# Splitting every second weight unit of the merged stage with ScalarE and an adding transfer in place of VectorE

## The chip, the cores and the metric

The kernel runs on one core of a Trainium2 chip. The metric is the device time of one execution in microseconds. The core has TensorE (PE in the profile, with its weight loads as PEld), VectorE (DVE), ScalarE (ACT), GpSimd (POOL) and SyncE (SP). Each works through its own queue of instructions in order, and they wait for each other through semaphores. Transfers are issued from a queue (here from SP's, ScalarE's or GpSimd's) and carried out by 16 DMA engines that all queues share.

## The reference

One decoder layer on 256 tokens of width 2048, all in float32. The part that matters here is the end, in which two branches are projected, gated and merged:

```python
h = _rmsnorm(x, pre_norm_g)
proj = jnp.einsum('bsd,de->bse', h, w_in)
...                                     # attention -> attn, short convolution -> conv
y_mla = jnp.einsum('bse,ed->bsd', attn, w_o_mla)
y_conv = jnp.einsum('bse,ed->bsd', b_gate * conv * jax.nn.silu(z_conv), w_o_conv)
merged = jax.nn.sigmoid(g_mla) * y_mla + jax.nn.sigmoid(g_conv) * y_conv
out = jnp.einsum('bsd,de->bse', merged, w_out)
x = x + _rmsnorm(out, post_norm_g)
```

g_mla and g_conv are column blocks of proj. The four products that make merged are each 256 x 2048 by 2048 x 2048.

## The kernel before

TensorE multiplies operands of the type float32r, a float32 that is rounded to fewer bits. To keep the precision each operand is split in two: hi is the rounded value and lo = value - hi, rounded too. A product is then three matmuls, hi times hi, hi times lo and lo times hi (`product`, line 227). Weights are split on the chip, once each.

Weights come in units, numbered in the order of their use (`plan`). A unit is 128 x 2048 float32, 1024 KB. `load_raw` issues its load on SP's queue into one of three raw buffers. `split_unit` splits it in two halves of 1024 columns: `split_act` (line 244) has ScalarE write hi (a copy with rounding, line 245) and VectorE write lo = raw - hi (line 246). The halves lie in five buffers for hi (tag whi) and five for lo (tag wlo). `ahead` and `take` keep loads up to three units and splits one unit ahead of the unit that TensorE uses; on the chip the buffers decide how far ahead the work really runs.

The merged stage is the loop `for c in range(4)` at line 967. For each block of 512 output columns c there are four products n: the two gates (left operand x_both, the normalised input), the attention branch (at_both) and the convolution branch (cv_both). Each product takes four units (`tokens`, line 941), and a unit serves both token tiles t and four slices k4 of 128 rows: first the four slices for t = 0, then the four for t = 1, 24 matmuls. The first half of a unit holds slices 0 and 1, the second half slices 2 and 3. In all 64 units (`u_d`), with the numbers 113 to 176. After n = 3 of each block VectorE gates and adds the two branches, transposes the result in blocks of 32, and GpSimd's queue writes it to device memory (eight DMAs far<-sg, line 328) and reads it back (two DMAs sg<-far, line 332), from where it is split into m_both, an operand of the last stage. The names of the tiles carry the unit: raw131 is the raw tile of unit 131, wlo131_1024 the low part of its second half.

TensorE's order is fixed by program order. Instructions inside `keep_in_program_order` keep theirs on their engine too; a scheduler places the others.

Of the kernel before, what the change touches and what calls it, by code (L numbers as in the profile page):

```python
# [11 lines left out]
F32 = mybir.dt.float32  # L12
F32R = mybir.dt.float32r
I32 = mybir.dt.int32
AF = mybir.ActivationFunctionType
ALU = mybir.AluOpType
# [66 lines left out]
def tile_layer(ctx: ExitStack, tc: tile.TileContext, xw, w0, xb, x, pos, pvec, post_g, wc, wz, wcv, wkr, wqk, wqr, wv, cwr, wsq, out):  # L83
    nc = tc.nc
# [21 lines left out]
    def add(ap, width=UNIT):  # L106
        plan.append((ap, width))
        return len(plan) - 1
# [30 lines left out]
    u_d = [[[add(wsq[n, c, k]) for k in range(4)] for n in range(4)] for c in range(4)]  # L139
# [3 lines left out]
    u_out = {ck: add(wsq[4, ck[0], ck[1]]) for ck in out_order}  # L143
# [4 lines left out]
    def load_raw(i):  # L148
# [16 lines left out]
        if i == u_ckv[1]:  # L165
            tc.keep_in_program_order(nc.sync.dma_start(out=x_tok, in_=x))

    def split_unit(i):
        t, w = raws.pop(i), plan[i][1]
        parts = []  # L170
        if i == u_kr:
            t = t[:, :w].rearrange("p (k c) -> p k c", k=KD)
            for h in range(2):
                both = wpool.tile([P, HALF], F32R, name=f"whi{i}_{h}", tag="whi", bufs=5)
                both = both[:, :].rearrange("p (k j c) -> p k j c", k=KD // 2, j=2)
                ks = slice(h * KD // 2, (h + 1) * KD // 2)
                split_act(both[:, :, 0], both[:, :, 1], t[:, ks])
                parts.append(both.rearrange("p k j c -> p k (j c)"))
            splits[i] = parts
            return  # L180
        if i <= u_qa[-1]:

            hi, lo = (wpool.tile([P, HALF], F32R, name=f"{o}{i}", tag=o, bufs=5) for o in ("whi", "wlo"))
            for j in range(2):
                k, o = 2 * i + j, j * XW
                src = x_first if k == 0 else t[:, o : o + S]
                split_scaled(x_both, src, k)
                split_act(hi[:, j * R : (j + 1) * R], lo[:, j * R : (j + 1) * R], t[:, o + S : o + XW], True)
            splits[i] = [(hi, lo)]
            return  # L190
        for h in range(0, w, HALF):
            n = min(HALF, w - h)
            if u_out[3, 0] <= i < u_out[3, 3]:
                hi, lo = (op.tile([P, HALF], F32R, name=f"w{o}{i}_{h}") for o in ("hi", "lo"))
            else:
                hi = wpool.tile([P, HALF], F32R, name=f"whi{i}_{h}", tag="whi", bufs=5)
                lo = wpool.tile([P, HALF], F32R, name=f"wlo{i}_{h}", tag="wlo", bufs=5)
            split_act(hi[:, :n], lo[:, :n], t[:, h : h + n], i == u_head[0][1], i in (u_grp["r", 0], u_grp["v", 0], u_head[0][0]))
            parts.append((hi, lo))
        splits[i] = parts  # L200

    def ahead(i, raw=3, split=1):
        while done["raw"] < min(i + raw, len(plan)):
            load_raw(done["raw"])
            done["raw"] += 1
        while done["split"] < min(i + 1 + split, len(plan)):
            while done["raw"] <= done["split"]:
                load_raw(done["raw"])
                done["raw"] += 1
            split_unit(done["split"])  # L210
            done["split"] += 1
# [32 lines left out]
    def split_act(hi, lo, src, keep=False, later=False):  # L244
        a = nc.scalar.activation(hi, src, AF.Copy)  # L245
        b = nc.vector.tensor_tensor(lo, src, hi.bitcast(F32), op=ALU.subtract)  # L246
        if keep:

            tc.keep_in_program_order(a)
        if keep or later:  # L250
            tc.keep_in_program_order(b)
# [52 lines left out]
    n = 2 * XW // S  # L304
# [38 lines left out]
    def split_scaled(dst, src, k):  # L343
        if k < 3:

            a = nc.vector.tensor_scalar(dst[:, k, :S], src, col("pre_g", k), None, op0=ALU.mult)
        else:
            a = nc.scalar.activation(dst[:, k, :S], src, AF.Copy, scale=col("pre_g", k))
        tc.keep_in_program_order(a)
        tc.keep_in_program_order(  # L350
            nc.vector.scalar_tensor_tensor(
                dst[:, k, S:], src, col("pre_g", k), dst[:, k, :S].bitcast(F32), op0=ALU.mult, op1=ALU.subtract
            )
        )
# [839 lines left out]
```

## Time and profile before

| | before |
|---|---|
| median of two runs | 1034.59 us (1034.59 and 1034.60) |
| span of the profiled execution | 1032.9 us |
| its time beside the span | 1.7 us of the run lie outside it |
| merged stage (589.95 to 938.15 us) | 348.20 us |
| mean granted clock of TensorE | 0.999 |
| VectorE, ScalarE, GpSimd busy in the merged stage | 192.78, 156.29, 22.24 us |
| DMA share in the merged stage | 0.58 |

Times are from the start of the span. A row of a timeline reads: start, duration, engine, line of the kernel, operation, out<-in, shapes, count, and in brackets the idle time ahead of it with what ended it. A row of waits reads: engine, what it was about to do, what it waited for, total us, times, longest. A row of DMA queues reads: packets, MB, share of the 16 engines' time; a row of DMA issues: what, from which queue, count, KB each, median us from issue to landing. The line numbers are those of the kernel before; in the changed kernel everything behind the change stands 11 lines further down.

### The profile page before, as it was taken

The numbers are of one execution on the slowest core, as the hardware profiler recorded it, in microseconds if no ns is written. First come the engines' busy times: TensorE is split into PE (matmuls) and PEld (weight loads), VectorE is DVE, ScalarE is ACT, GpSimd is POOL, SyncE is SP. The second block draws the span as 40 slices with busy tenths as digits, with TensorE's granted clock in tenths as the row PEclk, the third lists the DMA queues.
The fourth block names the chain that finished last, engine by engine and source line by source line (L and its number), as shares of the span: only waits on it lengthen the run. The fifth ranks groups of instructions, "written<-read, shape, count | busy, mean of one in ns | idle before, by whom it ended". The sixth has DMA issues, their size and how long they took to land.

```text
span 1032.9 us, 12670 instructions
## 1 busy us (share of the span) xinstructions
PE 1026.4 (99%) x4648; PEld 854.6 (83%) x4648; DVE 687.9 (67%) x973; ACT 531.3 (51%) x750; POOL 174.2 (17%) x324
## 2 busy tenths in 40 slices
PE   9999999999999999999999999999999999999997
PEld 8888888888888888888888888888888888888886
DVE  7588777787687777777777785564455455455562
ACT  7675555655456464564555465344434444443551
POOL 4620421104210223112133120020010001002000
PEclk9999999999999999999999999999999999999999
DMA  9775766558675676857676765565565556558642
GB/s 356 280 257 214 269 215 227 207 191 297 212 252 193 209 279 210 278 184 242 229 271 222 267 217 200 204 222 188 201 218 208 188 202 243 183 187 335 231 165 81
DMA packets 44669, 233.24 MB, mean 226 GB/s; under 512 B 7968, under 2 KB 10656, under 8 KB 21696
## 3 DMA queue, kind: packets, MB, share of 16 engines
q1 hardware_dynamic: 32544, 199.67, 54.4%
q0 software_dynamic: 11632, 29.48, 8.9%
q10 hardware_dynamic: 432, 3.29, 0.8%
q8 instruction: 36, 0.59, 0.2%
q14 instruction: 25, 0.20, 0.1%
HBM read 215.66 MB, written 12.58 MB: 221 GB/s over the span
## 4 chain that ended last, share of the span: by engine, by line
PE 99%; DVE 0%; ACT 0%; issue 0%
PE cv L88 34%; PE sq L88 34%; PE z L88 8%; PE out L88 8%; PE qa L88 2%; PE kn L88 2%; PE qn L88 2%; PE vv L88 2%; PE ckv L88 2%; PE qr L88 1%; PE o L88 1%; PE sw L88 1%; PE sc L88 1%; PE idle L88 0%; PE kr L88 0%; DVE og L1048 0%
## 5 line engine op out<-in xcount | busy, mean ns | idle before, releaser
L246 DVE TENSOR_TENSOR wlo<-raw,whi 128x1024 fp32r<-128x1024 f32 (+1 forms) x370 | 440.5, 1196 | 276.6 <-ACT whi L245 265.5
L245 ACT ACTIVATE whi<-raw 128x1024 fp32r<-128x1024 f32 (+1 forms) x372 | 382.7, 1035 | 412.2 <-PE sq L88 180.5
L88 PE MATMUL cv<-whi,x_both 128*128 128x512 f32 x1024 | 319.8, 389 | 0.0
L88 PEld LDWEIGHTS cv<-whi,x_both 128*128 128x128 f32 x1024 | 192.3, 188 | 39.6
L88 PE MATMUL cv<-wlo,x_both 128*128 128x512 f32 x512 | 199.4, 390 | 0.0
L88 PE MATMUL sq<-whi,x_both 128*128 128x512 f32 x512 | 158.2, 389 | 0.0
L88 PEld LDWEIGHTS sq<-whi,x_both 128*128 128x128 f32 x512 | 96.1, 188 | 19.8
L88 PEld LDWEIGHTS cv<-wlo,x_both 128*128 128x128 f32 x512 | 96.1, 188 | 19.3
L88 PE MATMUL sq<-wlo,x_both 128*128 128x512 f32 x256 | 99.6, 389 | 0.0
L88 PE MATMUL z<-whi,x_both 128*128 128x512 f32 x256 | 80.0, 389 | 0.0
L88 PE MATMUL sq<-whi,at_both 128*128 128x512 f32 x256 | 79.4, 389 | 0.0
L88 PE MATMUL sq<-whi,cv_both 128*128 128x512 f32 x256 | 79.4, 389 | 0.0
L88 PE MATMUL out<-whi,m_both 128*128 128x512 f32 x256 | 79.0, 389 | 0.0
L328 POOL DMA_DIRECT2D far<-sg x32 | 17.5, 553 | 305.8 <-DVE sg L320 232.6
L328 POOL DMA_DIRECT2D far<-via x64 | 35.2, 557 | 191.4 <-DVE via L320 190.0
L88 PEld LDWEIGHTS sq<-wlo,x_both 128*128 128x128 f32 x256 | 48.1, 188 | 10.0
L88 PEld LDWEIGHTS out<-whi,m_both 128*128 128x128 f32 x256 | 48.1, 188 | 10.0
L88 PEld LDWEIGHTS sq<-whi,cv_both 128*128 128x128 f32 x256 | 48.1, 188 | 9.9
L88 PEld LDWEIGHTS sq<-whi,at_both 128*128 128x128 f32 x256 | 48.1, 188 | 9.9
L88 PEld LDWEIGHTS z<-whi,x_both 128*128 128x128 f32 x256 | 48.1, 188 | 9.9
L88 PE MATMUL z<-wlo,x_both 128*128 128x512 f32 x128 | 49.8, 389 | 0.0
L88 PE MATMUL sq<-wlo,at_both 128*128 128x512 f32 x128 | 49.8, 389 | 0.0
(227 smaller groups left out, 1131.3 us busy)
## 6 DMA issues: line engine op xcount, KB each, us to landing
raw<-wsq_dram SPq DMA_DIRECT2D x80, 1024.0 KB, 4.8
raw<-wcv_dram SPq DMA_DIRECT2D x64, 1024.0 KB, 5.5
raw<-wz_dram SPq DMA_DIRECT2D x16, 1024.0 KB, 4.8
raw<-wqk_dram SPq DMA_DIRECT2D x8, 1024.0 KB, 6.1
cw<-cwr_dram POOLq DMA_DIRECT2D x24, 256.0 KB, 5.8
raw<-wc_dram SPq DMA_DIRECT2D x4, 1024.0 KB, 9.8
raw<-wv_dram SPq DMA_DIRECT2D x4, 1024.0 KB, 5.3
far<-via POOLq DMA_DIRECT2D x64, 48.0 KB, 4.1
```

What stands on the lines that cost most here:

```text
L88: return tc.keep_in_program_order(nc.tensor.matmul(*a, **kw))
L245: a = nc.scalar.activation(hi, src, AF.Copy)
L246: b = nc.vector.tensor_tensor(lo, src, hi.bitcast(F32), op=ALU.subtract)
L328: tc.keep_in_program_order(queue.dma_start(out=f[i], in_=m))
```

## The change

In the merged stage the units with an odd number (113, 115, ... 175, the first and third of each product) are split in another way. ScalarE writes hi as before, then a second ScalarE instruction writes lo = -hi, and a DMA from GpSimd's queue adds the raw columns onto lo within SBUF: lo = -hi + raw. VectorE has no part in it. The units with an even number and all other stages stay as they are. 

```diff
+    def by_transfers(i):
+
+        return u_d[0][0][0] <= i < u_out[0, 0] and i % 2 == 1
+
     def split_unit(i):
...
                 hi = wpool.tile([P, HALF], F32R, name=f"whi{i}_{h}", tag="whi", bufs=5)
                 lo = wpool.tile([P, HALF], F32R, name=f"wlo{i}_{h}", tag="wlo", bufs=5)
+            if by_transfers(i):
+                src = t[:, h : h + n]
+                nc.scalar.activation(hi[:, :n], src, AF.Copy)
+                nc.scalar.activation(lo[:, :n], hi[:, :n].bitcast(F32), AF.Copy, scale=-1.0)
+                tc.keep_in_program_order(nc.gpsimd.dma_start(out=lo[:, :n], in_=src, accum_op=ALU.add))
+                parts.append((hi, lo))
+                continue
             split_act(hi[:, :n], lo[:, :n], t[:, h : h + n], i == u_head[0][1], i in (u_grp["r", 0], u_grp["v", 0], u_head[0][0]))
             parts.append((hi, lo))
```

GpSimd's queue at the end of the first column block (c = 0, after unit 128) held only the writes and the reads back of the merged tiles before, from this block to the next:

```order
L328 DMA far_6181<-sg1_0_5883 32x4x128 x4
L328 DMA far_6185<-sg1_1_5885 32x4x128 x4
L332 DMA sg0_0_5733<-far_6181 128x512
L332 DMA sg0_1_5735<-far_6185 128x512
L328 DMA far_6765<-sg1_0_6480 32x4x128 x4
```

The same place now, with the adding transfers (line 206) of units 129 to 133 round it:

```order
L206 DMA wlo129_0_6163<-raw129_6126 128x1024
L206 DMA wlo129_1024_6168<-raw129_6126 128x1024
L339 DMA far_6199<-sg1_0_5893 32x4x128 x4
L339 DMA far_6203<-sg1_1_5895 32x4x128 x4
L343 DMA sg0_0_5739<-far_6199 128x512
L343 DMA sg0_1_5741<-far_6203 128x512
L206 DMA wlo131_0_6253<-raw131_6216 128x1024
L206 DMA wlo131_1024_6258<-raw131_6216 128x1024
L206 DMA wlo133_0_6323<-raw133_6286 128x1024
```

The transfers of units 131, 147 and 163 now stand behind the writes and reads back of a block, and those of units 129, 145 and 161 ahead of them.

ScalarE's queue in the same part of the program, before (units 128 to 130):

```order
L245 ACTIVATE whi128_1024_6116<-raw128_6076 128x1024
L245 ACTIVATE whi129_0_6146<-raw129_6110 128x1024
L245 ACTIVATE whi129_1024_6150<-raw129_6110 128x1024
L245 ACTIVATE whi130_0_6200<-raw130_6144 128x1024
L245 ACTIVATE whi130_1024_6204<-raw130_6144 128x1024
```

And now:

```order
L256 ACTIVATE whi128_1024_6132<-raw128_6090 128x1024
L204 ACTIVATE whi129_0_6162<-raw129_6126 128x1024
L205 ACTIVATE wlo129_0_6163<-whi129_0_6162 128x1024
L204 ACTIVATE whi129_1024_6167<-raw129_6126 128x1024
L205 ACTIVATE wlo129_1024_6168<-whi129_1024_6167 128x1024
L256 ACTIVATE whi130_0_6218<-raw130_6160 128x1024
L256 ACTIVATE whi130_1024_6222<-raw130_6160 128x1024
```

Each rounding of an odd unit is followed at once by its negated copy; the roundings of even units have moved back by as many instructions.

## The prediction

> **What bounds the kernel now.** I read the page's busy shares first, then the stretch of the merged stage, then its chain.
>
> ```profile
> PE 1026.4 (99%) x4648; PEld 854.6 (83%) x4648; DVE 687.9 (67%) x973; ACT 531.3 (51%) x750; POOL 174.2 (17%) x324
> ...
> 589.95:938.15 348.20, 348.20 (x1537) 288.38 (x1537) 192.78 (x190) 156.29 (x168) 22.24 (x41) 1.00 0.58 206
> ...
> 589.95 348.20 PE sq L88 x1536
> ```
>
> The first row is the page's: TensorE is busy for 99% of the span. The second is the stretch of the merged stage by engine (PE, PEld, DVE, ACT, POOL, then granted clock, DMA share, GB/s): TensorE is busy for all of its 348.20 us at clock 1.00, while VectorE has 155 us to spare in it. The third is the chain that ended last: the stage is one piece of TensorE work. So work taken off VectorE here cannot shorten anything. The stage has 64 units of weights (113 to 176), 24 matmuls each, so a unit lasts 348.20 / 64 = 5.44 us, and the question is only whether the new supply of the low parts arrives in time.
>
> ```profile
> ACT whi L245 <- PE sq L88: 180.2, 109, 3.0
> DVE wlo L246 <- ACT whi L245: 146.7, 70, 2.9
> ```
>
> These waits in the stage say how weights are paced: ScalarE waits for TensorE to give a buffer back, VectorE for ScalarE. There are five high and five low buffers of half a unit, so half n is rounded when half n-5 has been used. The rows round the start of unit 129 (first matmul at 676.87, where the right operand turns from cv_both to x_both) give the times:
>
> ```profile
> 675.71 1.06 ACT L245 ACTIVATE whi<-raw 128x1024 fp32r<-128x1024 f32 x1 [3.02 <-PE sq L88]
> 677.07 1.06 ACT L245 ACTIVATE whi<-raw 128x1024 fp32r<-128x1024 f32 x1 [0.30 <-PE sq L88]
> ...
> 676.80 1.23 DVE L246 TENSOR_TENSOR wlo<-raw,whi 128x1024 fp32r<-128x1024 f32 x1 [0.29 <-ACT whi L245]
> ...
> 676.87 0.39 PE L88 MATMUL sq<-whi,x_both 128*128 128x512 f32 x1
> 677.10 0.39 PE L88 MATMUL sq<-wlo,x_both 128*128 128x512 f32 x1
> ```
>
> Call t the start of unit u-2. The first half of unit u is rounded at t + 0.20 (677.07 - 676.87), the second at t + 4.28 (675.71 less 676.87 - 5.44 = 671.43). TensorE wants the low part of the first half with the second matmul of unit u, at t + 10.88 + 0.23 = t + 11.11, and that of the second half six matmuls later, at t + 12.47. Today VectorE is done 1.06 + 1.23 us after the start of the rounding, some 6 us early for the second half. That 6 us is all the cover there is.
>
> **The change part by part.** *Removed:* 64 VectorE subtractions of 1.23 us (32 units, two halves), 79 us, all beside TensorE: worth nothing, by the rows above.
>
> *Added on ScalarE:* 64 copies of 128 x 1024 at 1.06 us (the row of the rounding, same shape), 68 us on an engine that is busy 156 of 348 us. They stand right behind their rounding, which is on the path to the low part, so they count as latency. Behind such a copy waits the next half's rounding, due 1.44 us after that of the second half (5.44 + 0.20 - 4.28) and held up to about 2.1 us; it belongs to a unit that VectorE splits, with some 6 us to spare, so this delay stays hidden.
>
> *Added on GpSimd's queue:* 64 transfers of 512 KB within SBUF that read the raw half, read the low tile and write it. They go out at t + 0.20 + 2 x 1.06 + 0.1 = t + 2.4 (first half) and t + 4.28 + 2.12 + 0.1 = t + 6.5 (second half), 0.1 for two handovers (676.77 to 676.80 is one). What is left until TensorE wants them is 8.7 us and **6.0 us**. So the landing time of a second half decides, and no transfer that adds stands in the trace. Its neighbours, from the answer on DMA for this stage and the page's list of issues:
>
> ```profile
> q1 hardware_dynamic: 9223, 67.15, 54.4%
> q0 software_dynamic: 1664, 4.20, 3.7%
> ...
> raw<-wsq_dram SPq DMA_DIRECT2D x64, 1024.0 KB, 4.8
> ...
> sg<-far POOLq DMA_DIRECT2D x6, 256.0 KB, 5.3
> ...
> mv<-cv_f POOLq DMA_DIRECT2D x8, 254.0 KB, 5.6
> ```
>
> The nearest rows are GpSimd's own: 256 KB lands 5.3 us after its issue in this stage, and within SBUF 254 KB takes 5.6 us in the stage before. The lower bound is the raw load, 4.8 us for 1024 KB, on another queue. Engine time: q0 moved 4.20 MB in 3.7% of 348.2 us, 3.07 us for a MB of all 16 engines, so 512 KB (0.524 MB) take 1.6 us if only the source counts, and 3.2 us if the destination, which has to be read before it can be added to, counts as well. I take the second, since the sum needs both operands. Landing: 5.3 + 0.8 (the other 256 KB) + 1.6 (the destination's read) = 7.7, and 0.5 for sharing: per pair of units (10.88 us) the engines are busy 0.58 x 10.88 = 6.3 us and get 6.4 us more, which is over 100%, so some queueing is certain if the engine time is right. That makes **8.2 us**, with 4.8 and about 12 as ends (the upper one has both added terms twice as long, 5.3 + 2 x 2.4 = 10.1, and 2 for queueing). TensorE then pauses 8.2 - 6.0 = 2.2 us inside each such unit. Since every buffer is given back by TensorE itself, a pause moves all later releases with it and nothing is caught up: 32 x 2.2 = **70 us**. The oversubscribed engines say the same from the other side: (12.7 - 10.88) x 32 = 58 us at least.
>
> The Trainium skill, "Collectives: The Full Stack" (Stop 4, and "Why ReduceScatter is half of AllGather"), has it that an add inside the DMA engines costs nothing by itself but needs two source reads, which halves the rate. That is the 3.2 us taken above rather than 1.6; no run shows it so far.
>
> *Moved past on GpSimd's queue.* The transfers stand in one queue with the transposes of the merged tiles. At each of three boundaries (after units 128, 144, 160) the queue of the changed kernel has the eight writes, the two reads back, and only then the two transfers of units 131, 147, 163. Before:
>
> ```profile
> 677.11 2.20 POOL L328 DMA_DIRECT2D far<-sg  x4 [70.77 <-ACT whi L245]
> 681.40 2.17 POOL L328 DMA_DIRECT2D far<-sg  x4 [2.09 <-DVE sg L320]
> 684.21 0.57 POOL L332 DMA_DIRECT2D sg<-far  x1 [0.64 <-DMA far<-sg]
> 688.38 0.57 POOL L332 DMA_DIRECT2D sg<-far  x1 [3.60 <-DMA far<-sg]
> ```
>
> The second read back waits 3.60 us for the writes to land and leaves the queue at 688.95, 12.1 us after the start of unit 129. The first transfer of unit 131 is wanted 11.1 us after that start, so it is late before it is issued: 12.1 + 7.7 - 11.1 = 8.7 us, and about 1 us more for the second half behind it. Of these 9.7, 2.2 have already been spent by unit 129's own pause (the queue is tied to unit 128's end), and 2.2 are counted for unit 131: 5.3 extra, three times, **16 us**. At the start of the stage unit 115's second half stands behind writes that wait for VectorE, but the pause there is of the usual size, and I add nothing.
>
> *Raw buffers* are now held until the transfer has landed, so load u+3 is issued only then. There are three of them, so it serves an even unit, which VectorE splits quickly: it lands about t + 12.5 + 4.8 = t + 17.3 and its rounding is due at t + 5.44 x 3 + 0.2 = t + 16.5 (a pause moves both): 0.8 us late, or 2 to 3 beside the transfers, against 6 us of slack. Hidden. SP's next load behind it is for unit u+4, whose rounding is due 5.4 us later.
>
> **Sum:** 70 + 16 = 86 us. The profiled execution has a span of 1032.9 us; the two runs have 1034.59 and 1034.60, so 1.7 us lie outside the span. 1034.6 + 86 = **1121 us**.
>
> **Rivals.** A: *only the source counts.* The transfer lands after 5.3 + 0.8 = 6.1 us: pauses of 0.1 to 0.6 us, 3 to 19 us, and the boundaries cost 12.1 + 6.1 - 11.1 = 7.1, with the second half 7.6, times three, 23 us: 1061 to 1077, say **1066**. For it: the 254 KB copy within SBUF is hardly slower than 192 to 256 KB from elsewhere, so the fixed part seems large and the bytes cheap. Against: the sum needs the second read.
>
> B, **not slower:** *the landing is hidden.* If the transfers land in 5.9 us or less, no unit pauses in the steady run, and the boundaries cost three times landing + 1.0, at most 20.7 us, just 2%. At the raw load's 4.8 us it is 3 x 5.8 = 17 us: **1052**. For it: loads of 1024 KB do it. Against: every 256 KB on GpSimd's queue in this stage takes longer.
>
> The Trainium skill, "DMA: Bandwidth & Descriptors" (Anatomy of one DMA), would have it so: 2.0 us and bytes / 436 GB/s, an estimate of 3.2 us for 512 KB, hence 1034.6 + 3 x 4.2 = 1047. By that rule 256 KB would take 2.6 us; the trace has 5.3, and does not agree.
>
> C: *adding is slow.* If a transfer holds the engines twice as long as I take, 6.4 us, a pair of units needs 12.8 + 6.3 = 19.1 us of them in place of 10.88: 32 x 8.2 = 263 us, about **1300**. Nothing speaks for it but that no adding transfer is in the trace.
>
> D: *pauses cost the clock.* Now the clock is 1.00 throughout, and 0.96 only in the last stretch, the one with TensorE idle:
>
> ```profile
> 1000.00:1033.00 33.00, 27.18 (x120) 21.95 (x118) 10.75 (x20) 7.69 (x16) 0.00 (x0) 0.96 0.18 64
> ```
>
> If half a unit after each pause ran at half speed, each would cost 2.7 us more: 1121 + 87 = **1208**. The Trainium skill, "TensorE: Matmul & The Clock Gate" (Part 1), puts the drop behind an idle window of about 3.4 us; by that rule pauses of 2.2 us would not trigger it and only the three boundaries would.
>
> **How the numbers follow.** Forecast (1090 to 1170) 46%, A 24%, B 11%, C 12%, D 6%, faster 1%: with TensorE without a gap in the stage I find no mechanism that shortens it. The predicted time is the forecast's, 1121. The range goes from 1052 (B with the raw load's landing) to 1235 (landing near 11.5 us, or D); it leaves out C and the lower part of B, and that is under 2 in 10. About 2%, 20.7 us, is what a measurement of this kernel can tell from no change: faster 0.01, within 0.11, slower 0.88.
>
> **What would show it.** In the profile after: 64 transfers from raw to wlo on GpSimd's queue with a median landing near 8 us (A: 6, B: under 6, C: over 11); TensorE in the merged stage idle some 2 us per odd unit, waiting for that transfer, and 8 to 10 us in units 131, 147, 163; a stage of about 434 us in place of 348; a DMA share near 0.9; VectorE at some 114 us there; the stages on either side unchanged. A gapless TensorE in the stage, or pauses that wait for ScalarE and not for the transfers, would prove me wrong.

## The result and the profile after

The changed kernel takes 1129.26 us (1127.98 and 1130.54) against 1034.59: 1.0916 times the time before, 95% interval 1.0884 to 1.0947. The prediction was 1121, slower, in a range of 1052 to 1235. The profiled execution has a span of 1126.2 us and lies 1.8 us under its run of 1127.98.

The page's busy shares, the merged stage as one window (PE, PEld, DVE, ACT, POOL, clock, DMA share, GB/s), and the end of the chain in the kernel after:

```profile
PE 1046.1 (93%) x4648; PEld 854.0 (76%) x4648; DVE 611.5 (54%) x909; ACT 597.3 (53%) x814; POOL 230.2 (20%) x388
...
588.99:1030.99 442.00, 369.31 (x1541) 289.28 (x1540) 118.69 (x128) 220.84 (x230) 75.82 (x102) 0.97 0.86 238
...
1030.99 87.05 PE out L88 x384
```

The last stage's 384 matmuls take 87.05 us as before; the loss is all in the merged stage, which lasts 442 us in place of 348. VectorE has given up 74 us there (192.78 to 118.69), for nothing. TensorE was gapless and now is not: 442.0 less 369.3 leaves 72.7 us without a matmul, and over the page it is also busy 19.7 us longer for the same 4648 matmuls (1046.1 against 1026.4). These two make 92.4 of the 93.3 us by which the span grew.

The waits in the stage say what TensorE stood still for, and the rows on DMA how the transfers fared (queues, then issues with KB each and median us to landing):

```profile
PEld sq L88 <- DMA wlo<-raw: 94.0, 49, 10.4
PE sq L88 <- DMA wlo<-raw: 72.7, 46, 10.0
...
ACT whi L204 <- DMA raw<-wsq_dram: 24.3, 15, 3.1
```

```profile
q1 hardware_dynamic: 9356, 68.16, 44.5%
q0 software_dynamic: 10626, 36.78, 40.9%
...
raw<-wsq_dram SPq DMA_DIRECT2D x65, 1024.0 KB, 7.4
wlo<-raw POOLq DMA_DIRECT2D x62, 512.0 KB, 8.4
```

All 72.7 us are waits for the adding transfers. These land in 8.4 us by the median of the window (8.3 over all 64), and the raw loads have slowed from 4.8 to 7.4 us. From the q0 row a transfer holds the 16 engines for (0.409 x 442.0 - 12.9) / 62 = 2.7 us, where 12.9 us is what the other traffic on that queue took before.

TensorE's pauses in a stretch away from the block boundaries, from its timeline (in brackets the idle time):

```profile
766.84 0.50 PE L88 MATMUL sq<-wlo,at_both 128*128 128x512 f32 x1 [1.28 <-DMA wlo<-raw]
769.32 0.50 PE L88 MATMUL sq<-wlo,at_both 128*128 128x512 f32 x1 [0.82 <-DMA wlo<-raw]
780.17 0.50 PE L88 MATMUL sq<-wlo,cv_both 128*128 128x512 f32 x1 [1.05 <-DMA wlo<-raw]
782.90 0.50 PE L88 MATMUL sq<-wlo,cv_both 128*128 128x512 f32 x1 [1.07 <-DMA wlo<-raw]
```

Each odd unit pauses twice, once per half, about 2.1 us in all; from 769.32 to 782.90 a pair of units takes 13.58 us in place of 10.88.

And the last of the three boundaries, first GpSimd's queue, then TensorE in unit 163:

```profile
922.11 2.17 POOL L339 DMA_DIRECT2D far<-sg  x4 [0.45 <-DVE sg L331]
928.04 0.57 POOL L343 DMA_DIRECT2D sg<-far  x1 [3.77 <-DMA far<-sg]
931.01 0.56 POOL L343 DMA_DIRECT2D sg<-far  x1 [2.40 <-DMA far<-sg]
931.57 2.70 POOL L206 DMA_DIRECT2D wlo<-raw  x3
```

```profile
939.92 0.80 PE L88 MATMUL sq<-wlo,x_both 128*128 128x512 f32 x1 [10.01 <-DMA wlo<-raw]
```

The transfers go out the moment the second read back has left, at 931.57; the first lands 8.3 us later and TensorE has waited 10.01 us for it. Its first matmul takes 0.80 us instead of 0.39. This boundary is the longest of the three: the pauses in units 131, 147 and 163 add up to 4.8, 7.8 and 10.0 us.

### The profile page after: what moved, and what is told of

The parts are those of the page before. It is cut to its first block, busy times and chain, and to the rows that moved or that the text cites. A ratio compares the mean times of both kernels' runs of the same rounds, so it can differ in the third digit from the quotient of the medians.

```text
span 1126.2 us, 12857 instructions
## 1 busy us (share of the span) xinstructions
PE 1046.1 (93%) x4648; PEld 854.0 (76%) x4648; DVE 611.5 (54%) x909; ACT 597.3 (53%) x814; POOL 230.2 (20%) x388
## 4 chain that ended last, share of the span: by engine, by line
PE 69%; DMA 20%; issue 6%; DVE 2%; ACT 1%; POOL 1%; POOLq 0%; SPq 0%; ACTq 0%
PE cv L88 31%; DMA wlo<-raw 15%; PE sq L88 9%; PE z L88 8%; PE out L88 8%; DMA raw<-wsq_dram 3%; PE kn L88 2%; PE qa L88 2%; PE qn L88 2%; PE vv L88 2%; PE ckv L88 2%; DMA far<-sg 2%; PE qr L88 1%; PE sw L88 1%; PE o L88 1%
## 5 line engine op out<-in xcount | busy, mean ns | idle before, releaser
L257 DVE TENSOR_TENSOR wlo<-raw,whi 128x1024 fp32r<-128x1024 f32 (+1 forms) x306 | 362.4, 1192 | 378.6 <-ACT whi L256 372.7
L256 ACT ACTIVATE whi<-raw 128x1024 fp32r<-128x1024 f32 (+1 forms) x308 | 314.4, 1030 | 298.4 <-PE cv L88 122.5
L88 PE MATMUL sq<-whi,x_both 128*128 128x512 f32 x512 | 162.9, 399 | 0.0
L204 ACT ACTIVATE whi<-raw 128x1024 fp32r<-128x1024 f32 x64 | 67.8, 1059 | 148.9 <-PE sq L88 118.8
L88 PE MATMUL sq<-wlo,x_both 128*128 128x512 f32 x256 | 104.6, 409 | 41.2 <-DMA wlo<-raw 41.1
L206 POOL DMA_DIRECT2D wlo<-raw x64 | 55.4, 891 | 313.8 <-ACT wlo L205 299.1
L88 PEld LDWEIGHTS sq<-whi,x_both 128*128 128x128 f32 x512 | 99.1, 194 | 20.3
L205 ACT ACTIVATE wlo<-whi 128x1024 fp32r<-128x1024 f32 x64 | 67.7, 1059 | 1.9
L88 PE MATMUL sq<-wlo,cv_both 128*128 128x512 f32 x128 | 51.5, 402 | 15.2 <-DMA wlo<-raw 15.2
```

Source lines behind the costliest of these rows:

```text
L88: return tc.keep_in_program_order(nc.tensor.matmul(*a, **kw))
L204: nc.scalar.activation(hi[:, :n], src, AF.Copy)
L205: nc.scalar.activation(lo[:, :n], hi[:, :n].bitcast(F32), AF.Copy, scale=-1.0)
L206: tc.keep_in_program_order(nc.gpsimd.dma_start(out=lo[:, :n], in_=src, accum_op=ALU.add))
```

## The experiments

The theory: each pause is the landing of a transfer less its slack, the landing is long because the transfers and the raw loads share the DMA engines, and three boundaries of the queue add a pause of their own. The rivals: ScalarE's extra instruction, the fixed latency of GpSimd's queue, and the raw buffers that are held longer.

**ScalarE's part alone.**

```diff
-                tc.keep_in_program_order(nc.gpsimd.dma_start(out=lo[:, :n], in_=src, accum_op=ALU.add))
+                nc.vector.tensor_tensor(lo[:, :n], src, lo[:, :n].bitcast(F32), op=ALU.add)
```

> ScalarE's negated copy stays, but VectorE adds the raw columns to it in place of the transfer. Theory: ScalarE's extra 1.06 us per half is latency inside 6 us of slack and costs nothing: 1034.6 within 3 us. Rival: the second ScalarE instruction delays the roundings and evacuations behind it: 5 to 30 us of the 94 are its part.

Measured: 1034.79 us, ratio 1.0003 (0.9993 to 1.0012). The 64 extra ScalarE instructions are free; the transfer is the whole loss.

**The add taken away.**

```diff
-                tc.keep_in_program_order(nc.gpsimd.dma_start(out=lo[:, :n], in_=src, accum_op=ALU.add))
+                tc.keep_in_program_order(nc.gpsimd.dma_start(out=lo[:, :n], in_=src))
```

> The transfers copy the raw columns onto lo in place of adding them; everything that waits for them stays (lo is then the raw weight, so the low products are left without meaning; the time is that of the same instructions). Theory 1, the second read is a large part of the landing: without it a transfer of 512 KB holds the DMA engines 1.6 us (3.07 us per MB of the plain copies before) in place of 2.6, the median landing falls from 8.3 to about 6.5 us, the pauses inside the odd units nearly go and the three block boundaries stay: 1034.6 + 25 to 45 us, about 1070. Rival, the fixed latency of GpSimd's queue is the landing, and bytes hardly count: landing stays at 7.5 or more, 1110 to 1130.

Measured: 1072.28 us, ratio 1.037 (1.0343 to 1.0397). The q0 row of its merged stage (a window of 381 us), and the landing of its transfers:

```profile
q0 software_dynamic: 10601, 36.72, 26.8%
...
DMA to landing us min/median/max: 2.8/5.8/9.7
```

A copy holds the engines (0.268 x 381 - 12.9) / 62 = 1.4 us and lands in 5.8: the add costs 1.9 times the engine time for the same 512 KB, 2.5 us of landing, and 57 of the 95 us. What stays in this run is mostly the boundaries (its longest pauses are 5.0, 9.6 and 3.6 us, right behind them). Rival A's 1066 would have been a fair price, had only the source counted. The rival of a fixed latency, which had the landing stay at 7.5 us or more, falls.

**Units 131, 147 and 163 by VectorE.**

```diff
-        return u_d[0][0][0] <= i < u_out[0, 0] and i % 2 == 1
+        return u_d[0][0][0] <= i < u_out[0, 0] and i % 2 == 1 and i not in (131, 147, 163)
```

> Units 131, 147 and 163, whose transfers stand behind the writes and reads back of the merged tiles, are split by VectorE; the other 29 odd units stay with transfers. Theory: the three boundaries cost 5 us each beyond an ordinary pause plus that pause (2.2) and the slow clock after a long pause: 1129 less 22 to 40, about 1098. Rival: a boundary's pause only takes the place of ordinary pauses, because what waits there catches up: 1129 less 3 x 2.2 = 7 at most, above 1120.

Measured: 1105.35 us, ratio 1.0681 (1.0658 to 1.0704). The three units were 23.9 us of the loss, 8.0 each; the other 29 keep 70.8, that is 2.4 each. The pauses alone are 50.8 us in this run, 1.75 for each of the 29; the rest is TensorE busy longer (1046.0 us over the page against 1026.4).

**One half of each odd unit.** Two kernels, the first or the second half by a transfer, the other by VectorE:

```diff
-            if by_transfers(i):
+            if by_transfers(i) and h == 0:
```

```diff
-            if by_transfers(i):
+            if by_transfers(i) and h:
```

> Only the first half of each odd unit goes by a transfer, the second is split by VectorE. Theory 1, slack less landing decides: a first half has 8.7 us, with half the transfers the landing is about 7, so no pause in the steady run; the boundaries cost 12.1 + 7 - 11.1 = 8 us each: 1034.6 + 24, with slow clock up to 35: 1058 to 1070. Rival, each transfer costs whatever its slack, through the shared engines and the late raw loads: half of the 94 us, about 1080 or more.

> Only the second half of each odd unit goes by a transfer (6.0 us of slack). Theory 1, slack less landing decides: the landing is about 7 us with half the transfers, so a pause of about 1 us in 32 units, 32 us, and at the three boundaries 12.1 + 7 - 12.5 = 6.6 us, 20 us: about 1085. Theory 2, the oversubscribed engines decide: with one transfer per pair of units they are busy 6.3 + 2.6 = 8.9 of 10.88 us, the landing falls under 6 us and only the boundaries stay: about 1055.

Measured: first halves 1073.6 us, ratio 1.037 (1.033 to 1.041); second halves 1069.81, ratio 1.0339 (1.0322 to 1.0357). The landings, first halves above:

```profile
DMA to landing us min/median/max: 4.9/8.1/10.9
```

```profile
DMA to landing us min/median/max: 4.3/4.4/9.4
```

and all but one of the pauses of the run with second halves:

```profile
698.92 0.80 PE L88 MATMUL sq<-wlo,x_both 128*128 128x512 f32 x1 [8.50 <-DMA wlo<-raw]
...
796.49 0.79 PE L88 MATMUL sq<-wlo,x_both 128*128 128x512 f32 x1 [8.73 <-DMA wlo<-raw]
...
894.88 0.79 PE L88 MATMUL sq<-wlo,x_both 128*128 128x512 f32 x1 [8.91 <-DMA wlo<-raw]
```

This was not what either theory had in numbers. With one transfer per pair of units a second half lands in 4.4 us, inside its 6.0 us, so its steady run has next to no pause, as the theory of shared engines said; but the same transfer as a first half lands in 8.1. The total load does not make this difference: the DMA share is 0.76 with first halves (720 to 790 us) and 0.75 with second halves (710 to 785 us). The halves differ in when they go out, not in size. A raw load now waits for the landing of a transfer, the next load follows it within 0.4 to 0.8 us, and a first half goes out right behind such a pair (loads at 758.71 and 759.13, transfer at 760.24, landed 9.6 us later). A second half goes out behind most of it (loads at 753.76 and 754.55, transfer at 760.09, landed 4.8 us later). In flight at the issue were two raw loads for 21 of the 32 first halves, and never more than one for a second half.

Of the first halves' pauses, 23.2 us in the profiled run, 18.8 stand at the boundaries: 8.1 us of landing is still inside most of the 8.7 us of slack. The second halves' 35 us lie at the three boundaries, as the next run shows, 11.7 us each, more than the 6.6 expected.

The same run shows why the price of a boundary is more than its pause. Windows behind its first one (columns as above; the count in the first brackets is of TensorE's instructions):

```profile
690.00:695.00 5.00, 0.42 (x2) 0.00 (x0) 1.20 (x1) 0.00 (x0) 1.49 (x2) 1.00 0.80 238
695.00:698.90 3.90, 0.00 (x0) 0.00 (x0) 0.00 (x0) 0.00 (x0) 0.00 (x0) 0.54 0.77 165
698.90:702.00 3.10, 3.08 (x7) 2.48 (x8) 0.00 (x0) 0.00 (x0) 0.00 (x0) 0.50 0.64 201
702.00:705.00 3.00, 3.00 (x14) 2.41 (x13) 0.00 (x0) 1.75 (x2) 0.00 (x0) 0.98 0.34 142
```

After 8.5 us without work the granted clock is at 0.50 and stays there for about 3.1 us, in which 7 matmuls are done instead of 14: some 1.6 us lost at this boundary.

**Second halves without the boundary units.**

```diff
-        return u_d[0][0][0] <= i < u_out[0, 0] and i % 2 == 1
+        return u_d[0][0][0] <= i < u_out[0, 0] and i % 2 == 1 and i not in (131, 147, 163)
...
-            if by_transfers(i):
+            if by_transfers(i) and h:
```

> Second halves only, and units 131, 147 and 163 by VectorE: 29 transfers. Theory: the whole 35 us of the run with second halves alone were the three boundaries (two pauses' worth of queue, then half clock), and a transfer that lands in 4.4 us is hidden by 6.0 us of slack: 1034.6 within 4 us. Rival: second halves have a cost of their own beside the boundaries: above 1042.

Measured: 1035.63 us, ratio 1.0011 (1.0001 to 1.0021). The 29 transfers are hidden; their landings are

```profile
DMA to landing us min/median/max: 4.4/4.4/5.7
```

So 4.4 us is what an adding transfer of 512 KB takes where it meets little else (27 of the 29 met the tail of one raw load, on average 1.4 us of it), and the boundaries were all but some 1 us of the cost of the second halves.

**Every fourth unit.**

```diff
-        return u_d[0][0][0] <= i < u_out[0, 0] and i % 2 == 1
+        return u_d[0][0][0] <= i < u_out[0, 0] and i % 4 == 1
```

> Only every fourth unit (113, 117, ... 173) goes by transfers, both halves; no such unit stands right behind a block boundary. Theory 1, slack less landing decides: the landing inside such a unit stays near 8 us, since both its transfers still meet a raw load, and each of the 16 units pauses about 2 us: 1034.6 + 32, about 1067. Theory 2, the engines' total decides: over two pairs of units they are busy 12.6 + 5.2 = 17.8 of 21.8 us, queues drain in between, pauses stay under 0.5 us: 1035 to 1045.

Measured: 1039.31 us, ratio 1.0039 (1.0025 to 1.0053), 4.5 us over the runs beside it or 0.3 us per unit. The median landing is 6.1 us. The transfers are as large and stand as close together within their unit as in the changed kernel; only the engines have a pair of units to drain in between. So a landing of 8 us is no property of the transfer. It comes from what else the engines carry while the transfer is under way.

**The raw buffers set free.**

```diff
-                tc.keep_in_program_order(nc.gpsimd.dma_start(out=lo[:, :n], in_=src, accum_op=ALU.add))
+                held = x_both[:, h // 512 : h // 512 + 2, :].rearrange("p k c -> p (k c)").bitcast(F32)
+                tc.keep_in_program_order(nc.gpsimd.dma_start(out=lo[:, :n], in_=held, accum_op=ALU.add))
```

> The same 64 adding transfers of 512 KB, but they read a fixed tile (1024 columns of x_both) in place of the raw half, so a raw buffer is free as soon as ScalarE has rounded it and the next load need not wait for a landing (the low parts of the odd units are then not those of the weights; the instructions and waits are otherwise the same). Theory 1, the raw buffers held until the landing push the loads into the time of the next transfers, and the late loads hold up the rounding of odd units: without that most of the 50 us of steady pauses go and the boundaries stay, 1034.6 + 35 to 55, about 1080. Theory 2, the DMA engines simply have more work than the units give time for: pauses stay, above 1110.

Measured: 1134.22 us, ratio 1.0966 (1.0937 to 1.0995). The rows of its merged stage:

```profile
q0 software_dynamic: 10877, 37.71, 41.4%
...
raw<-wsq_dram SPq DMA_DIRECT2D x63, 1024.0 KB, 5.5
wlo<-x_both POOLq DMA_DIRECT2D x62, 512.0 KB, 7.4
```

The loads come back to 5.5 us and ScalarE no longer waits for them, and the time does not come back. TensorE's pauses fall only from 72.7 to 65.6 us. They are fewer and longer (36 in place of 46), and behind several of them, away from the boundaries too, the granted clock falls to 0.50 (from 627 to 630 us, behind a pause of 2.79 us, for one); TensorE is busy 12.9 us longer than in the changed kernel (1059.0 against 1046.1 over the page). So the held buffers are not the main cause: without them the transfers still land in 7.4 us beside the loads. What they cost at an unchanged clock, this run does not tell.

## Why the prediction was right

The direction and the size held (94.7 us slower, 86 forecast), and so did the mechanism: TensorE waits for landings that are longer than their slack, and for the queue at three boundaries. That the size came so close is in part luck. The forecast put all 86 us into pauses; the pauses were 72.7, and TensorE was busy 19.7 us longer, which the sum did not have. By its own steps:

- **Nothing to gain, and ScalarE's part free.** Right: 1034.79 us with ScalarE's instruction and VectorE's add. (One figure on the way is off without consequence: 5.44 + 0.20 - 4.28 is 1.36 us, not 1.44.)
- **Landing 8.2 us.** The total was right, 8.3 measured, but by luck: it was put together wrongly. I took 7.7 us for a transfer by itself, from the rows of 256 KB on GpSimd's queue, and 0.5 for sharing. Beside little else it takes 4.4, and the other 4 come from sharing. The rows I started from, 5.3 us for 256 KB, were no fixed price either: these reads back landed in 3.1 to 6.9 us in the trace of before, beside raw loads. That the sharing is what spread them is argued, not tried. So a second half is not late by nature, as the sum had it: it is hidden when the first half of its unit does not go this way too (1035.63 us, without the boundary units).
- **Engine time.** 3.2 us estimated with both reads, 2.7 measured; 1.6 for the copy, 1.4 measured. That an adding transfer has to be counted at about two copies is shown by the copy's run (57 us); that it is the destination's read and not the addition itself, no run here separates. The cross-check by the oversubscribed engines (0.58 x 10.88 + 2 x 2.7 = 11.7 us of work per 10.88) has the right sign, and the runs with fewer transfers bear out that sharing makes the landing. It gives only 0.8 of the 2.7 us by which a pair has grown, though, 26 us in place of the 58 forecast as the least, and the total alone does not decide: at the same DMA share a first half landed in 8.1 us and a second half in 4.4. How the remaining 1.9 split between queueing behind the raw loads and the order of the two transfers on their queue stays open.
- **Pauses of 2.2 us, 32 times, never caught up.** Away from the boundaries a unit cost 2.4 us, but only 1.75 of it is pause; the rest is TensorE busy longer. The pauses do not sit in the second half alone, as I wrote: both halves pause, about 1 us each. I had called the raw loads hidden; ScalarE in fact waits 24.3 us for them ahead of odd units, and the loads go out in pairs, close to the issue of a first half; both make the first halves late too. The run with free raw buffers shows that undoing this takes only 7.1 us off the pauses.
- **The queue at the boundaries.** 5.3 us extra and 2.2 of an ordinary pause, 7.5 each, were put there; taking those units out gave 8.0 each. The 12.1 us until the queue is free was read from rows of before, the landing of 7.7 us on top of it was the sum that was put together wrongly. The agreement is one of means: the pauses were 4.8, 7.8 and 10.0 us where 8 to 10 were expected in each, and the 8.0 has the half clock in it, which was not counted.
- **The clock.** I had it as rival D, for all pauses, at 6%. In the changed kernel it happens at the boundaries alone, and the clock is 1.00 throughout the stretch with pauses of 0.8 to 1.7 us, below. With second halves alone it is 0.50 for 3.1 us of work after 8.5 us without any. The Trainium skill, "TensorE: Matmul & The Clock Gate" (Part 1), has the drop behind an idle window of about 3.4 us. These two stretches agree with that, but other runs do not: in the run with units 131, 147 and 163 by VectorE the clock was 0.50 from 604.0 to 610.8 us and from 853.2 to 856.6, and the longest pauses just ahead were 2.12 and 2.07 us, while a pause of 2.98 us in the changed kernel (ended at 633.76) left it at 1.00. So a pause of 2 us can be enough, and its length alone does not tell.

```profile
750.00:805.00 55.00, 46.04 (x194) 35.51 (x194) 12.74 (x12) 27.41 (x28) 6.87 (x8) 1.00 0.86 234
```

- **TensorE busy 19.7 us longer**, which I had not counted. The matmuls at the boundaries that ran at a granted clock of 0.50 were busy 13.8 us in all, so half of that, some 7 us, is of the clock. The rest, some 0.3 us each, goes with the 46 pauses: the first matmul after one shows 0.50 us in place of 0.39, and the matmul before it no longer overlaps with a successor. That split is worked out, not tried by itself.

Rival B's page, "DMA: Bandwidth & Descriptors" of the Trainium skill, deserves a second look. Its 2.0 us and bytes / 436 GB/s give an estimate of 4.4 us when both reads are counted as bytes (1.05 MB), which is what the transfer takes here beside little else. That both reads count is my reading. For the copy, with one read, the same estimate is 3.2 us, and the quickest copy landed in 2.8. I had rejected the rule on a row that was taken beside raw loads; at a DMA share of 0.86 the landing of the adding transfer is twice the estimate.

## What to carry to other kernels

Before work is moved from an idle engine to transfers, add up what the DMA engines already carry per step of the bound engine: here 6.3 of 10.88 us were taken, one adding transfer per 10.88 us, issued behind most of a pair of raw loads, was free (0.1%), and two cost 7%, or 9% with the boundaries. Then look at what is in flight when the transfer goes out, since the sum does not tell that. A landing time read from a busy stage has that stage's sharing in it; it is not a fixed price, and the same transfer issued 4 us later landed in half the time. And a queue that carries an urgent transfer must hold nothing ahead of it that waits for another landing: three such places cost 24 of the 95 us.

## What the runs showed of the hardware

- An adding transfer of 512 KB within SBUF holds the 16 engines 1.9 times as long as a copy (2.7 against 1.4 us), and GpSimd issues it in 0.86 us where the copy takes 0.54:

```profile
L206 POOL DMA_DIRECT2D wlo<-raw x64: 842/861/1442, 582.3 to 1012.5; - x64
```

```profile
L206 POOL DMA_DIRECT2D wlo<-raw x64: 537/537/565, 584.0 to 957.1; - x64
```

The first row is the changed kernel's, the second the copy's (min/median/max in ns).

- Beside no more than the tail of a raw load that transfer lands in 4.4 us with little spread (4.4 to 5.7 over 29), less than the 5.3 us that 256 KB took on the same queue beside the raw loads before.
